# Batch norm with ReLU on one core: two-image tiles with 4 KB rows, or four tiles with 32 KB runs per partition

## The chip, the cores and the metric

The kernel runs on one core of one Trainium2 chip. The metric is the device time of one launch in microseconds (us), as the median over several runs. Beside that stands one profiled execution, whose span, from its first to its last instruction, is a little shorter than its device time.

## The reference

The input `x` has 32 images of 128 channels, each a plane of 32 by 32 float32 values (4 KB). Every channel has four parameters. In short:

```python
normalized = (x - running_mean[None, :, None, None]) / np.sqrt(running_var[None, :, None, None] + eps)
scaled = normalized * gamma[None, :, None, None] + beta[None, :, None, None]
return np.maximum(scaled, 0).astype(np.float32)
```

So each plane is multiplied by one number of its channel, another number of its channel is added, and negative values become zero. The input is 16.78 MB and the output is as large.

## The kernel before, in words

The 128 channels lie on the 128 partitions of the on-chip memory. A tile holds two images (1 MB, 8 KB per partition), and there are 16 tiles, all with a buffer of their own (`BUFS = 16`), so no load waits for a buffer. In DRAM one image is a block of 512 KB in which channel follows channel, so that a transfer of a tile moves 256 rows of 4 KB: two per partition, 512 KB apart, and neighbouring partitions are 4 KB apart.

Three queues issue transfers. GpSimd's (lines 63 to 66) brings the four parameter vectors, each as one row on one partition. The sync queue, SP, brings tile 0, in two halves, and then the tiles that ScalarE (ACT) does not bring: 2, 4, 6 and 8 to 15 (`emit_input`, line 58). ACT's own queue brings tiles 1, 3, 5 and 7 before ACT has anything to compute, and takes all the stores (lines 118 and 145). On a queue, transfers are issued in the order of the program; the Tile framework puts the waits on semaphores in, and hands the DMA semaphores out in turn, so that a transfer may also wait until an earlier one with the same semaphore has landed.

The parameter rows become columns through four small matmuls against a one (line 79). ACT takes the square root (line 89), and VectorE (DVE) makes from that the scale and the bias of each channel, as columns of 128 numbers (lines 97 to 103). Then the tiles go through ACT one by one: `relu(scale * x + bias)` in place, one instruction over both images of a tile (line 138), and its store behind it (line 145). Only tile 0 is done in three pieces (256 columns, 768 columns, then the second image; lines 109 and 118).

Of the kernel before, what the change touches and what calls it, by code (L numbers as in the profile page):

```python
# [1 line left out]

# [4 lines left out]


@with_exitstack
def kernel(  # L10
    ctx: ExitStack,
    tc: tile.TileContext,
    x: bass.AP,
    gamma: bass.AP,
    beta: bass.AP,
    running_mean: bass.AP,
    running_var: bass.AP,
    eps: bass.AP,
    out: bass.AP,
):  # L20
    nc = tc.nc

    B, C, H, W = x.shape
    HW = H * W
    assert C == nc.NUM_PARTITIONS, f"expected {nc.NUM_PARTITIONS} channels, got {C}"

    x3 = x.rearrange("b c h w -> b c (h w)")
    out3 = out.rearrange("b c h w -> b c (h w)")

    f32 = mybir.dt.float32  # L30

    NBMAX = 2
    n_tiles = B // NBMAX
    sizes = [NBMAX] * n_tiles
    scalar_tiles = (1, 3, 5, 7)
    splits = {0: 2, 1: 2}
    BUFS = 16
    SEPARATE_PSUM = True
    FIRST_PIECES = (256, HW - 256)

    params = ctx.enter_context(tc.tile_pool(name="params", bufs=1))
    eps_t = params.tile([C, 1], f32)
    nc.vector.memset(eps_t, float(eps))  # L43
    prow = params.tile([1, 4 * C], f32)
    one_t = params.tile([1, 1], f32)
    nc.vector.memset(one_t, 1.0)  # L46

    data = ctx.enter_context(tc.tile_pool(name="data", bufs=BUFS))
    tiles = {}
    for i in (0,) + scalar_tiles:  # L50
        tiles[i] = data.tile([C, NBMAX, HW], f32, name="t")

    def emit_input(i, t, engine):
        nsp = splits.get(i, 1)
        step = NBMAX // nsp
        b0 = i * NBMAX
        for j in range(nsp):
            engine.dma_start(  # L58
                out=t[:, j * step : (j + 1) * step],
                in_=x3[b0 + j * step : b0 + (j + 1) * step].transpose([1, 0, 2]),  # L60
            )

    nc.gpsimd.dma_start(out=prow[0:1, 3 * C : 4 * C], in_=running_var[None, :])  # L63
    nc.gpsimd.dma_start(out=prow[0:1, 0 * C : 1 * C], in_=gamma[None, :])  # L64
    nc.gpsimd.dma_start(out=prow[0:1, 2 * C : 3 * C], in_=running_mean[None, :])  # L65
    nc.gpsimd.dma_start(out=prow[0:1, 1 * C : 2 * C], in_=beta[None, :])  # L66

    emit_input(0, tiles[0], nc.sync)
    for i in scalar_tiles:
        emit_input(i, tiles[i], nc.scalar)  # L70

    pp = ctx.enter_context(tc.tile_pool(name="pp", bufs=1, space=bass.MemoryType.PSUM))
    if SEPARATE_PSUM:
        pcols = [pp.tile([C, 1], f32, name=f"p{k}") for k in range(4)]
    else:
        pc = pp.tile([C, 4], f32)
        pcols = [pc[:, k : k + 1] for k in range(4)]
    for k in (3, 0, 2, 1):
        nc.tensor.matmul(  # L79
            pcols[k],  # L80
            prow[0:1, k * C : (k + 1) * C],
            one_t[0:1, 0:1],
            start=True,
            stop=True,
        )
    g_col, b_col, mu_col, var_col = pcols

    std_t = params.tile([C, 1], f32)
    nc.scalar.activation(  # L89
        out=std_t,  # L90
        in_=var_col,
        func=mybir.ActivationFunctionType.Sqrt,
        bias=eps_t[:, 0:1],
        scale=1.0,
    )
    rstd_t = params.tile([C, 1], f32)
    nc.vector.reciprocal(out=rstd_t, in_=std_t)  # L97
    scale_t = params.tile([C, 1], f32)
    nc.vector.tensor_mul(out=scale_t, in0=g_col, in1=rstd_t)  # L99
    ms_t = params.tile([C, 1], f32)  # L100
    nc.vector.tensor_mul(out=ms_t, in0=mu_col, in1=scale_t)  # L101
    bias_t = params.tile([C, 1], f32)
    nc.vector.tensor_sub(out=bias_t, in0=b_col, in1=ms_t)  # L103

    out_ring = {}
    n_out = [0]

    def relu_store(t, b, img, c0, c1):
        nc.scalar.activation(  # L109
            out=t[:, img : img + 1, c0:c1],  # L110
            in_=t[:, img : img + 1, c0:c1],
            func=mybir.ActivationFunctionType.Relu,
            bias=bias_t[:, 0:1],
            scale=scale_t[:, 0:1],
        )
        eng = out_ring.get(n_out[0], nc.scalar)
        n_out[0] += 1
        eng.dma_start(
            out=out3[b : b + 1, :, c0:c1].transpose([1, 0, 2]),
            in_=t[:, img : img + 1, c0:c1],  # L120
        )

    for i, nb in enumerate(sizes):
        b0 = i * NBMAX
        if i in tiles:
            t = tiles.pop(i)
        else:
            t = data.tile([C, NBMAX, HW], f32, name="t")
            emit_input(i, t, nc.sync)
        if i == 0:  # L130
            c0 = 0
            for w in FIRST_PIECES:
                relu_store(t, b0, 0, c0, c0 + w)
                c0 += w
            for img in range(1, nb):
                relu_store(t, b0 + img, img, 0, HW)
        else:
            nc.scalar.activation(  # L138
                out=t[:, :nb],
                in_=t[:, :nb],  # L140
                func=mybir.ActivationFunctionType.Relu,
                bias=bias_t[:, 0:1],
                scale=scale_t[:, 0:1],
            )
            nc.scalar.dma_start(out=out3[b0 : b0 + nb].transpose([1, 0, 2]), in_=t[:, :nb])  # L145


# [1 line left out]
_INS = ['x', 'gamma', 'beta', 'running_mean', 'running_var', 'eps']  # L149
_OUTS = [((32, 128, 32, 32), 'float32')]  # L150
#: Inputs that are plain numbers.
_NUMBERS = {'eps': 1e-05}


# [26 lines left out]
```

## Time and profile before

| | |
|---|---|
| median of 16 runs | 86.61 us (86.34 to 87.12) |
| the profiled execution: device time | 86.48 us |
| the profiled execution: span | 84.7 us |
| read from DRAM, written to it | 16.78 MB, 16.78 MB |
| mean rate of the DMA engines over the span | 396 GB/s |
| ACT busy | 34.8 us (41%) |
| PE, DVE, POOL busy | 2.3, 0.7, 2.2 us |

The profile names engines: PE is TensorE, DVE is VectorE, ACT is ScalarE, POOL is GpSimd, SP is SyncE; a q behind a name means the sequencer of that engine, which issues transfers and handles waits. A core has 16 DMA engines. "DMA share" is the time that packets took in a stretch, divided by the stretch and by 16; it may exceed 1 where records of packets overlap. q1 is SP's queue, q10 that of ACT, q0 that of GpSimd, q14 brings instructions. "L138" is line 138 of the kernel.

### The profile page before, as it was taken

The numbers are of one execution on the slowest core, as the hardware profiler recorded it, in microseconds if no ns is written. First come the engines' busy times: TensorE is split into PE (matmuls) and PEld (weight loads), VectorE is DVE, ScalarE is ACT, GpSimd is POOL, SyncE is SP. The second block draws the span as 40 slices with busy tenths as digits, with TensorE's granted clock in tenths as the row PEclk, the third lists the DMA queues.
The fourth block names the chain that finished last, engine by engine and source line by source line (L and its number), as shares of the span: only waits on it lengthen the run. The fifth ranks groups of instructions, "written<-read, shape, count | busy, mean of one in ns | idle before, by whom it ended". The sixth has DMA issues, their size and how long they took to land.

```text
span 84.7 us, 153 instructions
## 1 busy us (share of the span) xinstructions
PE 2.3 (3%) x8; PEld 2.0 (2%) x8; DVE 0.7 (1%) x6; ACT 34.8 (41%) x20; POOL 2.2 (3%) x8
## 2 busy tenths in 40 slices
PE   0006400000000000000000000000000000000000
PEld 0005300000000000000000000000000000000000
DVE  0001100000000000000000000000000000000000
ACT  0321479006920890000039598693987920000000
POOL 5500000000000000000000000000000000000000
DMA  1999999999999999999999999999999999999991
GB/s 25 321 389 417 410 426 404 412 418 408 403 392 418 422 418 428 418 420 422 418 429 416 422 420 418 429 416 420 424 416 429 416 422 420 416 429 418 420 422 64
DMA packets 9025, 33.57 MB, mean 396 GB/s; under 512 B 704, under 2 KB 832, under 8 KB 9024
## 3 DMA queue, kind: packets, MB, share of 16 engines
q10 hardware_dynamic: 5616, 20.97, 60.9%
q1 hardware_dynamic: 3280, 12.58, 36.9%
q0 software_dynamic: 128, 0.00, 0.1%
q14 instruction: 1, 0.01, 0.0%
HBM read 16.78 MB, written 16.78 MB: 396 GB/s over the span
## 4 chain that ended last, share of the span: by engine, by line
DMA 65%; ACT 7%; ACTq 4%; issue 3%
DMA t<-in_x_dram 65%; ACT t L138 7%; ACTq L58 2%; ACTq L145 2%
## 5 line engine op out<-in xcount | busy, mean ns | idle before, releaser
L138 ACT ACTIVATE t<-t,bias_t,scale_t 128x2048 f32<-128x2048 f32 x15 | 30.6, 2085 | 24.8 <-DMA t<-in_x_dram 22.4
L109 ACT ACTIVATE t<-t,bias_t,scale_t 128x256 f32<-128x256 f32 (+2 forms) x3 | 2.8, 950 | 2.2 <-DVE bias_t L103 1.7
L89 ACT ACT_TABLE_LOAD x1 | 1.3, 1283 | 3.5 <-issue 3.5
L79 PE MATMUL p<-one_t,prow 1*128 1x1 f32 x8 | 2.3, 354 | 7.2 <-DMA prow<-in_running_var_dram 7.1
L79 PEld LDWEIGHTS p<-one_t,prow 1*128 1x128 f32 x8 | 2.0, 306 | 7.4 <-issue 7.1
L89 ACT ACTIVATE std_t<-p,eps_t 128x1 f32<-128x1 f32 x1 | 0.3, 262 | 2.9 <-PE p L79 2.9
L63 POOL DMA_DIRECT2D prow<-in_running_var_dram x1 | 0.6, 617 | 0.8 <-POOLq L162 0.8
L64 POOL DMA_DIRECT2D prow<-in_gamma_dram x1 | 0.5, 484 | 0.0
L65 POOL DMA_DIRECT2D prow<-in_running_mean_dram x1 | 0.5, 484 | 0.0
L66 POOL DMA_DIRECT2D prow<-in_beta_dram x1 | 0.5, 484 | 0.0
L97 DVE RECIPROCAL rstd_t<-std_t 128x1 f32<-128x1 f32 x1 | 0.2, 165 | 7.1 <-ACT std_t L89 7.1
L103 DVE TENSOR_TENSOR bias_t<-p,ms_t 128x1 f32<-128x1 f32 x1 | 0.2, 159 | 0.4 <-PE p L79 0.4
L101 DVE TENSOR_TENSOR ms_t<-p,scale_t 128x1 f32<-128x1 f32 x1 | 0.2, 157 | 0.5 <-PE p L79 0.5
L99 DVE TENSOR_TENSOR scale_t<-p,rstd_t 128x1 f32<-128x1 f32 x1 | 0.2, 159 | 0.1
L162 POOL MEMSET const-float32-0.0<- 128x1 f32 x1 | 0.1, 98 | 0.2 <-issue 0.2
L162 POOL MEMSET const-bfloat16-1.0<- 128x1 bf16 x1 | 0.1, 101 | 0.0
L162 POOL MEMSET const-float32-1.0<- 128x1 f32 x1 | 0.1, 98 | 0.0
L162 POOL MEMSET const-uint8-127<- 128x1 uint8 x1 | 0.1, 98 | 0.0
L43 DVE MEMSET eps_t<- 128x1 f32 x1 | 0.1, 59 | 0.8 <-PEq L162 0.8
L46 DVE MEMSET one_t<- 1x1 f32 x1 | 0.1, 59 | 0.0
## 6 DMA issues: line engine op xcount, KB each, us to landing
out_dram<-t ACTq DMA_DIRECT2D x15, 1024.0 KB, 15.0
t<-in_x_dram SPq DMA_DIRECT2D x11, 1024.0 KB, 17.5
t<-in_x_dram ACTq DMA_DIRECT2D x3, 1024.0 KB, 16.7
t<-in_x_dram SPq DMA_DIRECT2D x2, 512.0 KB, 6.1
t<-in_x_dram ACTq DMA_DIRECT2D x2, 512.0 KB, 6.4
out_dram<-t ACTq DMA_DIRECT2D x1, 512.0 KB, 10.8
out_dram<-t ACTq DMA_DIRECT2D x1, 384.0 KB, 16.4
out_dram<-t ACTq DMA_DIRECT2D x1, 128.0 KB, 15.4
```

The lines of the kernel that those rows point to most:

```text
L58: engine.dma_start(out=t[:, j * step : (j + 1) * step], in_=x3[b0 + j * step : b0 + (j + 1) * step].transpose([1, 0, 2]),)
L63: nc.gpsimd.dma_start(out=prow[0:1, 3 * C : 4 * C], in_=running_var[None, :])
L64: nc.gpsimd.dma_start(out=prow[0:1, 0 * C : 1 * C], in_=gamma[None, :])
L65: nc.gpsimd.dma_start(out=prow[0:1, 2 * C : 3 * C], in_=running_mean[None, :])
L66: nc.gpsimd.dma_start(out=prow[0:1, 1 * C : 2 * C], in_=beta[None, :])
L79: nc.tensor.matmul(pcols[k], prow[0:1, k * C : (k + 1) * C], one_t[0:1, 0:1], start=True, stop=True,)
L89: nc.scalar.activation(out=std_t, in_=var_col, func=mybir.ActivationFunctionType.Sqrt, bias=eps_t[:, 0:1], scale=1.0,)
L97: nc.vector.reciprocal(out=rstd_t, in_=std_t)
L109: nc.scalar.activation(out=t[:, img : img + 1, c0:c1], in_=t[:, img : img + 1, c0:c1], func=mybir.ActivationFunctionType.Relu, bias=bias_t ...
L138: nc.scalar.activation(out=t[:, :nb], in_=t[:, :nb], func=mybir.ActivationFunctionType.Relu, bias=bias_t[:, 0:1], scale=scale_t[:, 0:1],)
L145: nc.scalar.dma_start(out=out3[b0 : b0 + nb].transpose([1, 0, 2]), in_=t[:, :nb])
L162: nc = _bacc.Bacc("TRN2", target_bir_lowering=False, num_devices=1)
```

## The change

The tensor is seen as 4096 rows of 4 KB (image by image, channel by channel). A block of 2048 rows is dealt out so that each partition holds 16 neighbouring rows: partition p of block t holds rows 2048t + 16p to 2048t + 16p + 15, which are 64 KB in one piece of DRAM. There are two blocks, and each is handled in two pieces of 8 rows per partition. That makes four tiles of 4 MB, with one run of 32 KB per partition each; neighbouring partitions are 64 KB apart in DRAM. All four loads are issued first, all on SP's queue; the four stores are issued on SP's queue too, each behind the computation of its tile.

A partition now holds 16 different channels (8 of them in each tile), the same 16 for every eighth partition. So the scale and the bias are tables of 128 by 16. The four parameter vectors are loaded as 8 rows of 16 numbers on ACT's queue, one matmul against an 8 by 128 matrix of zeros and ones (built by GpSimd, lines 67 and 68) spreads them over the 128 partitions, and square root, reciprocal, multiplications and subtraction work on 16 columns. ACT then does one instruction per row index, 8 per tile and 32 in all, with a column of the tables each.

Beside that, there is a transfer on ACT's queue near the start, which writes zeros to the first 512 bytes of each of the 32 images of the output (`fill`). The stores write over them later.

The core of the diff; the lines taken out are the body of the function shown above:

```diff
+J = 16
+PIECES = ((0, 8), (8, 16))
...
+    xr = x.rearrange("b c h w -> (b c) (h w)").rearrange("(t p j) w -> t p j w", p=P, j=J)
+    outr = out.rearrange("b c h w -> (b c) (h w)").rearrange("(t p j) w -> t p j w", p=P, j=J)
...
+    tiles = []
+    for t in range(T):
+        for a, b in PIECES:
+            xt = data.tile([P, b - a, HW], F32, name=f"x{t}_{a}")
+            nc.sync.dma_start(out=xt, in_=xr[t, :, a:b, :])
+            tiles.append((t, a, b, xt))
+    fill = params.tile([B, 128], F32, name="fill")
+    nc.vector.memset(fill, 0.0)
+    nc.scalar.dma_start(out=out.rearrange("b c h w -> b (c h w)")[:, 0:128], in_=fill)
+    raw = params.tile([Q, 4, J], F32, name="raw")
+    for k, src in enumerate((running_var, gamma, running_mean, beta)):
+        nc.scalar.dma_start(out=raw[:, k, :], in_=src.rearrange("(q j) -> q j", j=J))
+    eps_t = params.tile([P, 1], F32, name="eps_t")
     nc.vector.memset(eps_t, float(eps))
+    rep = params.tile([Q, P // Q, Q], F32, name="rep")
+    nc.gpsimd.memset(rep, 1.0)
+    nc.gpsimd.affine_select(
...
+    cols = psum.tile([P, 4, J], F32, name="cols")
+    nc.tensor.matmul(
+        cols.rearrange("p k j -> p (k j)"),
+        rep.rearrange("q r s -> q (r s)"),
+        raw.rearrange("q k j -> q (k j)"),
...
+    nc.scalar.activation(out=std_t, in_=cols[:, 0, :], func=ACTF.Sqrt, bias=eps_t[:, 0:1], scale=1.0)
...
+    for t, a, b, xt in tiles:
+        for j in range(a, b):
+            nc.scalar.activation(
+                out=xt[:, j - a, :],
+                in_=xt[:, j - a, :],
+                func=ACTF.Relu,
+                bias=bias_t[:, j : j + 1],
+                scale=scale_t[:, j : j + 1],
             )
...
+        nc.sync.dma_start(out=outr[t, :, a:b, :], in_=xt)
```

On SP's queue the whole program is shown here as a difference, the lines before with a minus and those after with a plus (the number behind a tile's name tells its buffer; "x11" is eleven alike in a row; the branches are the program's ends):

```order
-L58 DMA t<-in_x_dram 128x1024 x2
-L58 DMA t<-in_x_dram 128x2x1024 x11
-L176 UNCONDITIONAL_BRANCH
+L136 UNCONDITIONAL_BRANCH
+L50 DMA x_0_64<-in_x_dram 128x8192
+L50 DMA x_8_66<-in_x_dram 128x8192
+L50 DMA x_0_68<-in_x_dram 128x8192
+L50 DMA x_8_70<-in_x_dram 128x8192
+L105 DMA out_dram<-x_0_64 128x8192
+L105 DMA out_dram<-x_8_66 128x8192
+L105 DMA out_dram<-x_0_68 128x8192
+L105 DMA out_dram<-x_8_70 128x8192
```

Thirteen loads of up to 1 MB have become four of 4 MB, and the stores, which ACT issued, now stand behind the loads on this queue.

On ACT, at the start of the program before, with the semaphores that each instruction waits for in brackets (DMAHW0 to 7 count landings of transfers, the others count instructions of an engine):

```order
1 L58 DMA t<-in_x_dram 128x1024 x2
2 L58 DMA t<-in_x_dram 128x2x1024 x3
3 L89 ACT_TABLE_LOAD
4 L89 ACTIVATE std_t<-p_88,eps_t 128x1 [waits PE_49]
5 L109 ACTIVATE t<-t,bias_t,scale_t 128x256 [waits DMAHW0_49,DVE_49]
6 L109 ACTIVATE t<-t,bias_t,scale_t 128x768
7 L118 DMA out_dram<-t 128x256 [waits DMAHW2_49,Activation_49]
8 L118 DMA out_dram<-t 128x768 [waits DMAHW3_49,Activation_49]
9 L109 ACTIVATE t<-t,bias_t,scale_t 128x1024
10 L138 ACTIVATE t<-t,bias_t,scale_t 128x2048 [waits DMAHW1_49]
```

And on ACT now, from its first transfer to the second tile:

```order
1 L63 DMA raw<-in_running_var_dram 8x16
2 L57 DMA out_dram<-fill 32x128 [waits DVE_49]
3 L63 DMA raw<-in_gamma_dram 8x16
4 L63 DMA raw<-in_running_mean_dram 8x16
5 L63 DMA raw<-in_beta_dram 8x16
6 L86 ACT_TABLE_LOAD [waits DVE_49]
7 L86 ACTIVATE std_t<-cols,eps_t 128x16 [waits PE_49]
8 L98 ACTIVATE x_0_64<-x_0_64,bias_t,scale_t 128x1024 [waits DMAHW1_49,DVE_49]
9 L98 ACTIVATE x_0_64<-x_0_64,bias_t,scale_t 128x1024 x7
10 L98 ACTIVATE x_8_66<-x_8_66,bias_t,scale_t 128x1024 [waits DMAHW6_49]
```

ACT's large loads are gone, five small transfers stand in their place, and between the activations there is no store any more.

On SP after the change the waits of the last load and of the stores are these (the order of SP with its semaphores, rows 3 to 8):

```order
3 L50 DMA x_0_68<-in_x_dram 128x8192
4 L50 DMA x_8_70<-in_x_dram 128x8192 [waits DMAHW0_49]
5 L105 DMA out_dram<-x_0_64 128x8192 [waits DMAHW2_49,DMAHW1_49,Activation_49]
6 L105 DMA out_dram<-x_8_66 128x8192 [waits DMAHW6_49,Activation_49]
7 L105 DMA out_dram<-x_0_68 128x8192 [waits DMAHW7_49,DMAHW3_49,Activation_49]
8 L105 DMA out_dram<-x_8_70 128x8192 [waits DMAHW4_49,DMAHW0_49,Activation_49]
```

The fourth load waits for one small transfer whose semaphore it takes over, and the first store waits for the fill, for the first load and for ACT.

More of the change, by code (lines that the diff above doesn't have):

```diff
@@ L6 @@
 from concourse._compat import with_exitstack
+F32 = mybir.dt.float32
+ACTF = mybir.ActivationFunctionType
+J = 16
+PIECES = ((0, 8), (8, 16))
 @with_exitstack
@@ L24 @@
     HW = H * W
[L25 to L39, printed above, removed]
-    params = ctx.enter_context(tc.tile_pool(name="params", bufs=1))
@@ L42 @@
-    eps_t = params.tile([C, 1], f32)
-    nc.vector.memset(eps_t, float(eps))
[L44 to L60, printed above, removed]
-            )
@@ L63 @@
[L63 to L145, printed above, removed]
+    P = nc.NUM_PARTITIONS
@@ new lines @@
+    assert C % J == 0 and P % (C // J) == 0 and (B * C) % (P * J) == 0
+    Q = C // J
+    T = B * C // (P * J)
+    xr = x.rearrange("b c h w -> (b c) (h w)").rearrange("(t p j) w -> t p j w", p=P, j=J)
+    outr = out.rearrange("b c h w -> (b c) (h w)").rearrange("(t p j) w -> t p j w", p=P, j=J)
+    data = ctx.enter_context(tc.tile_pool(name="data", bufs=1))
+    params = ctx.enter_context(tc.tile_pool(name="params", bufs=1))
+    psum = ctx.enter_context(tc.tile_pool(name="psum", bufs=1, space=bass.MemoryType.PSUM))
@@ new lines @@
+    eps_t = params.tile([P, 1], F32, name="eps_t")
+    nc.vector.memset(eps_t, float(eps))
+    rep = params.tile([Q, P // Q, Q], F32, name="rep")
+    nc.gpsimd.memset(rep, 1.0)
+    nc.gpsimd.affine_select(
+        out=rep,
+        in_=rep,
+        compare_op=mybir.AluOpType.is_equal,
+        fill=0.0,
+        base=0,
+        pattern=[[0, P // Q], [-1, Q]],
+        channel_multiplier=1,
+    )
+    cols = psum.tile([P, 4, J], F32, name="cols")
[3 more added lines that the diff above has]
+        raw.rearrange("q k j -> q (k j)"),
+        start=True,
+        stop=True,
+    )
@@ new lines @@
+    std_t = params.tile([P, J], F32, name="std_t")
+    nc.scalar.activation(out=std_t, in_=cols[:, 0, :], func=ACTF.Sqrt, bias=eps_t[:, 0:1], scale=1.0)
+    rstd_t = params.tile([P, J], F32, name="rstd_t")
+    nc.vector.reciprocal(out=rstd_t, in_=std_t)
+    scale_t = params.tile([P, J], F32, name="scale_t")
+    nc.vector.tensor_mul(out=scale_t, in0=cols[:, 1, :], in1=rstd_t)
+    ms_t = params.tile([P, J], F32, name="ms_t")
+    nc.vector.tensor_mul(out=ms_t, in0=cols[:, 2, :], in1=scale_t)
@@ L149 @@
+    bias_t = params.tile([P, J], F32, name="bias_t")
+    nc.vector.tensor_sub(out=bias_t, in0=cols[:, 3, :], in1=ms_t)
+    for t, a, b, xt in tiles:
[6 more added lines that the diff above has]
+                scale=scale_t[:, j : j + 1],
+            )
+        nc.sync.dma_start(out=outr[t, :, a:b, :], in_=xt)
 _INS = ['x', 'gamma', 'beta', 'running_mean', 'running_var', 'eps']
```

## The prediction

> **What bounds the kernel now.** I read the page first: its busy shares, its 40 slices and its queues.
>
> ```profile
> PE 2.3 (3%) x8; PEld 2.0 (2%) x8; DVE 0.7 (1%) x6; ACT 34.8 (41%) x20; POOL 2.2 (3%) x8
> DMA  1999999999999999999999999999999999999991
> GB/s 25 321 389 417 410 426 404 412 418 408 403 392 418 422 418 428 418 420 422 418 429 416 422 420 418 429 416 420 424 416 429 416 422 420 416 429 418 420 422 64
> q10 hardware_dynamic: 5616, 20.97, 60.9%
> q1 hardware_dynamic: 3280, 12.58, 36.9%
> ```
>
> No compute engine is busy for half of the span. The DMA engines are full in every slice but the first and the last: the kernel is a stream of 33.55 MB through 16 engines. A wait of ACT or SP matters only if it leaves the engines without work, and none does. So the next question is where the stream starts and ends, and how fast it is in between. This view cuts the span into stretches; the last two columns are the DMA share and GB/s.
>
> ```profile
> 0.00:1.85 1.85, 0.00 (x0) 0.00 (x0) 0.08 (x2) 0.00 (x0) 0.81 (x6) 1.00 0.00 0
> 1.85:5.00 3.15, 0.00 (x0) 0.00 (x0) 0.00 (x0) 1.28 (x1) 1.43 (x4) 1.00 0.94 321
> 5.00:23.00 18.00, 2.27 (x8) 1.98 (x8) 0.64 (x4) 8.18 (x7) 0.00 (x0) 1.00 1.03 411
> 23.00:27.00 4.00, 0.00 (x0) 0.00 (x0) 0.00 (x0) 0.90 (x1) 0.00 (x0) 1.00 1.04 406
> 27.00:60.00 33.00, 0.00 (x0) 0.00 (x0) 0.00 (x0) 17.18 (x9) 0.00 (x0) 1.00 1.02 421
> 60.00:83.20 23.20, 0.00 (x0) 0.00 (x0) 0.00 (x0) 7.28 (x4) 0.00 (x0) 1.00 1.01 415
> 83.20:84.70 1.50, 0.00 (x0) 0.00 (x0) 0.00 (x0) 0.00 (x0) 0.00 (x0) 1.00 0.00 0
> ```
>
> Nothing moves for 1.85 us, then the stream lasts 81.35 us, then 1.50 us pass until the program ends. Taking 421 GB/s as the full rate, the stream loses 3.15 x 100/421 = 0.75 us while it gets going, 22 us x 11/421 = 0.57 us between 5 and 27 us (about 410), and 23.2 x 6/421 = 0.33 us at the end, where the engines run out one after another. The remaining 79.7 us are 33.55 MB at 421.
>
> **What sets 421 GB/s.** Short windows in which a queue moves packets of one size give the price of a packet. Here are, with packets, MB and share of 16 engines, ACT's queue from 23.5 to 24.6 us (its packets under 2 KB are the 1 KB pieces of tile 0's first store, and one of 4 bytes), the same queue from 69.1 to 69.6 us (4 KB packets alone), and the instruction queue from 70.2 to 70.3 us, which moves one packet of 8 KB:
>
> ```profile
> DMA packets 173, 0.44 MB, mean 400 GB/s; under 512 B 1, under 2 KB 87, under 8 KB 173
> q10 hardware_dynamic: 87, 0.09, 22.6%
> q10 hardware_dynamic: 49, 0.20, 97.4%
> q14 instruction: 1, 0.01, 19.3%
> ```
>
> 1 KB: 0.226 x 16 x 1100 ns / 86 = 46.2 ns. 4 KB: 0.974 x 16 x 500 / 49 = 159.0 ns. 8 KB: 0.193 x 16 x 100 = 309 ns. The first two give 37.6 ns per KB and 8.6 ns per packet whatever its size; 8 KB by that would be 309.4 ns, and is 309. So a packet has a fixed part, and up to 8 KB it doesn't come back with size. In wall time it is smaller, because records overlap:
>
> ```profile
> DMA packets 3274, 12.62 MB, mean 421 GB/s; under 512 B 192, under 2 KB 192, under 8 KB 3274
> q10 hardware_dynamic: 1638, 6.32, 51.3%
> q1 hardware_dynamic: 1636, 6.31, 51.2%
> ```
>
> From 30 to 60 us, 3082 packets of 4 KB and 192 tiny ones use 16 x 30 us: 155.7 ns per 4 KB packet with its part of the tiny ones, about 155.3 without. The fixed part in wall time is thus 155.3 - 4 x 37.6 = 4.9 ns, 3% of the time.
>
> **The change part by part.** *32 KB runs.* If a run travels as one packet, it costs 8 x 150.4 + 4.9 = 1208 ns, or 1212 with the whole 8.6. Each engine then moves 64 runs in place of 512 rows: 64 x 1209 = 77.4 us (77.3 to 77.6) in place of 79.7. No packet above 8 KB is in this trace, so this reaches four times further than the rows; the bound on the other side is the packet price of today, 79.7 us, below as a rival.
>
> *Start and end.* SP issues its first load where it did, so 1.85 us stay, and 1.50 us at the end, where no line changes. Getting going: from 0 (long runs flow at once) to 0.75 us as now; I take 0.7, as today's row is the nearest. The end: engines run out within part of a run, 0 to 1.2 us; I take today's 0.3.
>
> *Loads first, then stores.* Until 23 us the kernel before only loads, at 411 GB/s, and from then on stores are mixed in, and it soon does 421. Now loads run alone for half the stream. If the slower loads are a matter of bytes, 36.7 us of stream lose 36.7 x 11/421 = 1.0 us; if of packets, an eighth, 0.1. I take 0.45.
>
> *Small transfers.* The fill is 32 pieces of 512 B, two per engine at 8.6 + 18.8 = 27 ns; the parameters are 32 pieces of 64 B at some 11 ns on some engines. With the packets that close a transfer I take 0.15 us (0.05 to 0.25).
>
> *The tables, hidden.* The small transfers share the engines with 32 KB runs. From 5.3 to 8.3 us three queues were active:
>
> ```profile
> q1 hardware_dynamic: 173, 0.63, 52.5%
> q10 hardware_dynamic: 163, 0.59, 48.8%
> q0 software_dynamic: 128, 0.00, 2.4%
> ```
>
> They take turns packet by packet, whatever the size (above, 86 packets of 4 KB beside 87 of mostly 1 KB say the same). q0's 128 packets for four transfers on 16 engines are two per transfer and engine, one with data, one that closes it. So ACT's five small transfers queue at most 11 packets on an engine (four of 2, and the fill with 3), each letting one run of 1.21 us pass: the last parameter lands at about 1.85 + 13.3 + 1 = 16 us (1 for the landing itself, since the 1.50 us at the program's end hold a landing and the shutdown). From the first matmul to the bias took 2.5 us:
>
> ```profile
> 7.11 2.33 PE L79 MATMUL p<-one_t,prow 1*128 1x1 f32 x8 [7.11 <-DMA prow<-in_running_var_dram]
> 9.48 0.16 DVE L103 TENSOR_TENSOR bias_t<-p,ms_t 128x1 f32<-128x1 f32 x1 [0.40 <-PE p L79]
> L109 ACT ACTIVATE t<-t,bias_t,scale_t 128x1024 f32<-128x1024 f32 x1 | 1.2, 1239 | 0.4 <-ACT t L109 0.4
> 0.74 13.39 SPq L58 DMA_DIRECT2D t<-in_x_dram  x6
> ```
>
> With one matmul in place of four and 16 columns in place of one I keep 2.5: tables at 19 us. A tile is 8 activations, at most 8 x 1.24 = 9.9 us: the tiles are ready at 29, 39, 49 and 59 us. The loads end at 1.85 + 0.7 + 0.45 + 38.7 = 41.7 us. A transfer issued to idle engines starts 1.1 us later (0.74 to 1.85), so store 0 is needed by 40.6, then one every 9.7 us: 50, 60, 69. The cover is 11 us at every store. GpSimd's two instructions for the matrix have until 16 us, when the last parameter lands, and work beside that. The fourth load waits on SP for running_var's landing, at about 5 us, with the stores queued behind it; three loads, 29 us of work, cover that. The first store waits for the fill, long landed.
>
> *Sum.* Stream: 77.4 + 0.7 + 0.45 + 0.15 + 0.3 = 79.0 us. Span: 1.85 + 79.0 + 1.50 = 82.35. The device time of the profiled execution is 86.48 - 84.7 = 1.78 us above its span, which gives 84.1 us against 86.48; the median is 0.13 above that execution, which I leave in the rounding.
>
> **The rivals.** *The runs are cut up, or long packets gain nothing* (the change doesn't do what it says): 79.7 us of payload return, with 0.75, 0.57 and 0.33, and the time is 86.4, no change. For it: no run over 8 KB was seen. Against: the 8 KB packet lies on the line. The Trainium skill, page "DMA: Bandwidth & Descriptors", section "Specifications", puts line rate at 512 bytes and above, by which 4 KB rows have nothing to gain. The 46.2 and 159.0 ns rows contradict that: per byte the 1 KB packet is 16% dearer. The same page, "Why small descriptors are slow (HBM only)", names a fixed cost of about 3 cycles per packet, which has the form the rows show.
>
> *Streams that collide in DRAM* (slower). Before, a transfer covers one or two solid blocks of 512 KB; now the engines walk at a time through runs that start multiples of 64 KB apart, up to 8 MB. If such starts share parts of the memory, every packet stretches. Break-even is 33.55 MB in 81.35 - 0.7 - 0.3 - 0.15 = 80.2 us, 418 GB/s. The worst full slice behind the start, 389, gives 86.2 us of payload, 87.4 of stream and 92.5 us. For it: loads are already slower than the rest, 411. Against: from 27 to 60 us loads and stores walk blocks far apart in two tensors at once, and the rate is a flat 421, which the packet price explains alone. The Trainium skill, same page, section "Latency and other measured facts", speaks against the change here: copies whose partitions lie 4 MiB apart run at half rate (103 of 214 GB/s), those 512 KiB apart at 207. At 64 KB the page lists nothing; the halving would make an estimate of some 163 us, and no run here shows any.
>
> *Tables too late* (slower). If the small packets let more than one run pass per turn, store 0 misses its slot. At two runs the last parameter lands at 29.5, tile 0 is ready at 41.9, 1.3 us late, 85.4 us. At three it is 55.2, 14.6 us late, 98.7 us. It decides at just above two. For it: no row has a small packet beside long ones. Against: the turns above are one by one for 1 KB beside 4 KB and 32 bytes beside 4 KB.
>
> **How the numbers follow.** Forecast 0.76: 84.1 us, with own bounds, in the order of the sum, of 82.6 (77.3, 0, 0.1, 0.05, 0) to 85.9 (77.6, 0.75, 1.0, 0.25, 1.2). Cut or no gain 0.10: 86.4. Collisions 0.08: about 92.5. Late tables 0.04: 85 to 99. The rest, 0.02, I leave to what I don't see. The range is 82.6 to 86.4: the forecast and the case of no gain, about 0.82. A measurement of this kernel can tell about 0.2%, 0.17 us, from no change. Faster by more: the forecast and a third of the no-gain case, whose tiny packets also shrink in number, 0.79. Within: 0.07. Slower: 0.14, collisions, late tables and the rest.
>
> **What would show it.** Right: the queue table has some 1024 packets of 32 KB on SP's queue, priced near 1212 ns; the slices show about 433 GB/s in the store half and 422 to 433 in the load half; the first data packet is at 1.85 us and no slice between is empty; tables by 19 us; the first store issued near 29 us. Wrong: packets of 4 KB again, a rate of 421 or under, a hole near 42 us, or ACT still at work when its store's turn comes.

## The result, and the profile after

The change makes the kernel about 2% faster: 84.78 us (9 runs, 84.56 to 84.93) against 86.58 (48 runs), a ratio of 0.9785 with a 95% interval of 0.9769 to 0.9801. Forecast were 84.1 us in a range of 82.6 to 86.4. The profiled execution took 85.04 us with a span of 83.3.

From the page of the kernel after, the DMA row of the slices, its rate and the queues (packets, MB, share of 16 engines):

```profile
DMA  7789998998999799899879999999999999989970
GB/s 189 299 363 415 488 425 346 503 488 362 409 503 456 315 488 488 377 393 503 252 330 425 488 409 393 472 456 409 393 488 409 409 456 488 393 377 488 456 315 0
q1 hardware_dynamic: 1152, 33.55, 95.5%
q10 hardware_dynamic: 112, 0.02, 0.1%
```

The 8320 data packets of 4 KB and less have become 1024 of 32 KB with 128 small ones that close the eight transfers. A packet now lasts over half a slice and its bytes count where it starts, so the rate jumps between slices; only the dip in the two at 40 to 44 us (252, 330) is more than that. Longer stretches are steadier (last two columns: DMA share, GB/s):

```profile
0.00:1.80 1.80, 0.00 (x0) 0.00 (x0) 0.17 (x2) 0.00 (x0) 0.79 (x6) 1.00 0.00 0
1.80:5.00 3.20, 0.00 (x0) 0.00 (x0) 0.00 (x0) 1.28 (x1) 0.00 (x0) 1.00 1.10 389
5.00:38.00 33.00, 0.66 (x2) 0.50 (x2) 0.78 (x4) 20.50 (x19) 0.00 (x0) 1.00 1.01 437
38.00:44.00 6.00, 0.00 (x0) 0.00 (x0) 0.00 (x0) 6.00 (x7) 0.00 (x0) 1.00 0.95 322
44.00:80.00 36.00, 0.00 (x0) 0.00 (x0) 0.00 (x0) 10.07 (x9) 0.00 (x0) 1.00 1.00 432
82.00:83.30 1.30, 0.00 (x0) 0.00 (x0) 0.00 (x0) 0.00 (x0) 0.00 (x0) 1.00 0.00 0
```

The stream runs from 1.8 to 82.0 us, 80.2 us in place of 81.35. Loads, up to 38 us, and stores, behind 44, both move about 433 GB/s (437 and 432, with packets counted where they start); between them the rate falls to 322. The price of a packet there comes from SP's queue in three windows: 1.8 to 5 us, 38 to 44 and 44 to 80 (16 of the 75 packets and 48 of the 523 are the small ones, at 9 ns):

```profile
q1 hardware_dynamic: 38, 1.25, 109.9%
q1 hardware_dynamic: 75, 1.93, 94.8%
q1 hardware_dynamic: 523, 15.56, 100.1%
```

From 44 to 80 us, 475 long packets share 1.001 x 16 x 36 = 576.6 us: 1.213 us each. From 38 to 44 us, 59 long packets have 91.0 us where they should need 71.6: 19.3 us more, or 1.2 us on each of the 16 engines. I call this surplus over the regular price, per engine, the loss of a stretch. Followed packet by packet, it sits in the last two load runs of every engine (numbers 31 and 32 of 32), 1.2 to 2.2 us long and 1.8 in the mean; the first store run behind them has the regular price. At the start, 38 packets lose 0.64 us per engine in the same way.

The tables, from the timeline of after:

```profile
15.78 0.66 PE L78 MATMUL cols<-raw,rep 8*128 8x64 f32 x2 [15.78 <-DMA raw<-in_beta_dram]
17.77 36.30 ACT L98 ACTIVATE x<-x,bias_t,scale_t 128x1024 f32<-128x1024 f32 x32 [1.02 <-DVE bias_t L94]
26.95 27.48 SPq L105 DMA_DIRECT2D out_dram<-x  x4
```

The last parameter landed at 15.8 us and the tables were there at 17.8, late beside the 9.7 of before but without harm: the first store was issued at 26.95 us, and the engines began it at about 42.

### The profile page after: what moved, and what is told of

It is laid out like the page before. It is cut to its first block, busy times and chain, and to the rows that moved or that the text cites. A ratio compares the mean times of both kernels' runs of the same rounds, so it can differ in the third digit from the quotient of the medians.

```text
span 83.3 us, 117 instructions
## 1 busy us (share of the span) xinstructions
PE 0.7 (1%) x2; PEld 0.5 (1%) x2; DVE 1.0 (1%) x6; ACT 37.9 (45%) x34; POOL 0.8 (1%) x6
## 4 chain that ended last, share of the span: by engine, by line
ACT 43%; DMA 16%; ACTq 3%; DVE 1%; PE 1%; issue 1%; DVEq 0%
ACT x L98 42%; DMA raw<-in_beta_dram 16%; ACTq L63 2%; ACTq L136 1%; PE cols L78 1%; ACTq L57 0%; ACT std_t L86 0%; DVE rstd_t L88 0%; DVE ms_t L92 0%; DVE scale_t L90 0%; DVE bias_t L94 0%; DVEq L90 0%
## 5 line engine op out<-in xcount | busy, mean ns | idle before, releaser
L98 ACT ACTIVATE x<-x,bias_t,scale_t 128x1024 f32<-128x1024 f32 x32 | 36.3, 1226 | 1.0 <-DVE bias_t L94 1.0
L78 PE MATMUL cols<-raw,rep 8*128 8x64 f32 x2 | 0.7, 428 | 15.8 <-DMA raw<-in_beta_dram 15.8
L78 PEld LDWEIGHTS cols<-raw,rep 8*128 8x128 f32 x2 | 0.5, 308 | 15.7 <-issue 15.7
```

The source lines that it names most:

```text
L78: nc.tensor.matmul(cols.rearrange("p k j -> p (k j)"), rep.rearrange("q r s -> q (r s)"), raw.rearrange("q k j -> q (k j)"), start=True, s ...
L98: nc.scalar.activation(out=xt[:, j - a, :], in_=xt[:, j - a, :], func=ACTF.Relu, bias=bias_t[:, j : j + 1], scale=scale_t[:, j : j + 1],)
```

## The experiments

Each kernel is the one after the change with one edit. Its time is a median, its ratio is to the kernel before on the same chip.

**e1: without the early zeros.** Is the loss near 40 us the price of touching the output first, which the zeros might lower?

```diff
-    nc.scalar.dma_start(out=out.rearrange("b c h w -> b (c h w)")[:, 0:128], in_=fill)
```

> The early transfer of zeros is left out, nothing else. After the change each DMA engine's first two store packets take 1.8 us instead of 1.21, about 1.2 us in all, near 39 us. Theory 'first touch' (the first writes to the output are slow whoever makes them, and the zeros take part of that cost early): without the zeros the first store packets get dearer by some 0.5 us or more, and the time goes from 84.8 to 85.3 or more. Theory 'turn' (an engine that goes from loads to stores with nothing else to do pays for the change of direction): the zeros do nothing for it, the first two packets stay at 1.8 us and the time at 84.6 to 84.8. Both expect the tables some 3.6 us earlier (three packets fewer on ACT's queue ahead of beta, each behind a run of 1.21 us), at no gain in time.

84.75 us, ratio 0.9767 (0.9730 to 0.9803): nothing lost, nothing gained, where "first touch" expected 85.3 or more. (The expectation takes the slow runs for stores; they are the last loads, as said above.) From 38 to 44 us its SP queue shows:

```profile
q1 hardware_dynamic: 78, 2.03, 100.2%
```

62 long packets have 96.2 us against 75.2: 1.3 us per engine, as with the zeros. The zeros are dead weight.

**e2: 4 KB packets, all else kept.** A gap of 16 bytes behind each row in the tile cuts the runs.

```diff
-            xt = data.tile([P, b - a, HW], F32, name=f"x{t}_{a}")
+            xt = data.tile([P, b - a, HW + 4], F32, name=f"x{t}_{a}")[:, :, 0:HW]
```

> Each 4 KB row gets 16 bytes of padding in the on-chip tile, so that a partition's 32 KB are moved as 8 packets of 4 KB; addresses in DRAM, transfers, queues and tables stay. Theory 'packet price' (the prediction's: 4.9 ns of wall time per packet): 512 packets per engine in place of 64 cost 448 x 4.9 ns = 2.2 us more, so 87.0 us, slower than the kernel before, and the store half runs at 421 GB/s. Rival (the gain comes from the single queue, the pattern of 64 KB in DRAM or the order, not from run length): 84.8 us again. Both expect the table to be ready earlier, as the small packets pass 4 KB packets.

86.46 us, ratio 0.9962 (0.9939 to 0.9985). On the same chip e1 took 84.75 us, so run length is worth 1.7 us. Everything else together (single queue, order, tables) is worth the rest, 0.3 us by this ratio (0.1 to 0.5). Packets and rates of e2 from 10 to 38, 38 to 44 and 44 to 80 us, each as a total and as SP's queue:

```profile
DMA packets 2859, 11.51 MB, mean 411 GB/s; under 512 B 48, under 2 KB 48, under 8 KB 2859
q1 hardware_dynamic: 2859, 11.51, 102.5%
q1 hardware_dynamic: 622, 2.48, 102.6%
DMA packets 3753, 15.18 MB, mean 422 GB/s; under 512 B 48, under 2 KB 48, under 8 KB 3753
```

Stores do 422, the packet price, as forecast. Loads do 411: 2811 packets of 4 KB have 459.2 us against 446.9 at 159 ns, a loss of 0.75 us spread over the load half. But the 1.2 us before the first store are missing (0.1 between 38 and 44). So the sum is 84.78 + 2.2 + 0.75 - 1.1 = 86.6, near the 86.46 measured; my 87.0 had counted on the loss staying.

**e3: more changes between loads and stores.** The fourth load goes behind the first store.

```diff
         nc.sync.dma_start(out=outr[t, :, a:b, :], in_=xt)
+        if n == 0:
+            lt, la, lb, lx = tiles[3]
+            nc.sync.dma_start(out=lx, in_=xr[lt, :, la:lb, :])
```

> The fourth load is issued behind the first store: three loads, store, load, three stores, all on SP's queue. That makes three changes of direction in place of one. Theory 'turn': two changes from loads to stores at 1.2 us each and one back, of 0 to 0.7 us: time 86.0 to 86.7, with slow packets near 31 us, near 41 us and near 51 us. Theory 'first touch': only the first store pays, now near 31 us, and the time stays at 84.8.

85.01 us, ratio 0.9793 (0.9755 to 0.9831), 0.2 us above "first touch" and 1 below "turn". SP's queue from 28 to 34 us, the first change, and from 48 to 54, the last one:

```profile
q1 hardware_dynamic: 78, 2.03, 97.7%
q1 hardware_dynamic: 96, 2.62, 101.7%
```

The first change loses 1.15 us per engine (62 long packets), the last one 0.03 (80). "Turn" falls: the price is paid once, wherever the first store comes. "First touch" had that right, but e1 speaks against it, the slow packets are loads, and e8 below will speak against it too.

**e4: stores on ACT's queue.** Engines then take turns between a load run and a store run.

```diff
-        nc.sync.dma_start(out=outr[t, :, a:b, :], in_=xt)
+        nc.scalar.dma_start(out=outr[t, :, a:b, :], in_=xt)
```

> The stores go to ACT's queue, loads stay on SP's. From about 28 us on an engine then takes turns between a load run and a store run, as the kernel before did with its 4 KB rows. Theory 'turn': a store's slow start lies beside load packets of the other queue, the 1.2 us are hidden at least by half, time 83.6 to 84.2. Theory 'first touch': the first store packets hold the engine just as long, time 84.7 to 84.9. ACT has its four store issues of some 0.4 us more to do, which is covered.

85.34 us, ratio 0.9826 (0.9785 to 0.9867), slower than either theory gave. The loss is not hidden behind the other queue's packets (27 to 32 us; q1 loads, q10 the first stores):

```profile
q1 hardware_dynamic: 36, 1.18, 75.7%
q10 hardware_dynamic: 13, 0.43, 19.7%
```

49 long packets have 76.3 us against 59.4, 1.05 per engine. It is unevenly spread here: three engines have a single load run of 2.8 to 3.2 us. Followed to the end, the same three finish last, at 81.7, 82.1 and 82.3 us, and the other 13 by 81.25; in the kernel after the last one ends at 82.0. So these three make the stream 0.4 us longer, of the 0.6 by which the profiled execution is above that of the kernel after (85.64 against 85.04); the rest stays open.

**e6: short packets in the first store.** Tile 0 is stored as eight transfers of 4 KB rows.

```diff
+        if t == 0 and a == 0:
+            for r in range(a, b):
+                nc.sync.dma_start(out=outr[t, :, r, :], in_=xt[:, r - a, :])
+        else:
+            nc.sync.dma_start(out=outr[t, :, a:b, :], in_=xt)
```

> The store of the first tile goes out as eight transfers of one 4 KB row per partition; everything else keeps its 32 KB runs. So far: on every engine the last two load runs ahead of the first store take 1.8 us in place of 1.21 (about 1.2 us in all); the first store itself runs at full price; a later change from loads to stores costs nothing; 4 KB packets show no such stretch. Theory 'read ahead by packets' (an engine starts to read the next two packets while the last loads still arrive, and what it reads early is two whole runs): with 4 KB packets behind the loads the stretch shrinks to 0.3 us or less, at 0.3 us more for the packet price of 64 short packets: 83.9 to 84.2 us. Theory 'once' (the first store of the program costs 1.2 us whatever its packets are): 85.0 to 85.1 us, and the last two load runs are as slow as before.

85.10 us, ratio 0.9824 (0.9808 to 0.9839): "once". From 38 to 42.3 us SP's queue of e6 has

```profile
q1 hardware_dynamic: 32, 1.05, 82.6%
```

32 load runs at 0.826 x 16 x 4.3 / 32 = 1.78 us in the mean, exactly two per engine. The size of the store's packets doesn't matter.

**e8: a full-size store early.** One run of 32 KB of zeros per engine replaces the short rows.

```diff
-    fill = params.tile([B, 128], F32, name="fill")
+    fill = params.tile([16, 8192], F32, name="fill")
...
+    nc.scalar.dma_start(out=outr[0, 0:16, 0:8, :].rearrange("p j w -> p (j w)"), in_=fill)
```

> In place of the 32 short rows the early transfer writes one run of 32 KB of zeros per engine (16 partitions), behind the parameters on ACT's queue, so a full-size store passes each engine before 16 us. It moves 0.52 MB more, 1.21 us per engine. Theory 'once' (each engine pays 1.2 us the first time that a long store stands behind loads, and never again): slow load runs before 16 us, none near 39 us, time 84.8 + 1.2 = 86.0 us. Theory 'turn' (an engine that has been loading alone pays at the turn): the stretch near 39 us stays at 1.1 to 1.3 us, and the early one may come on top: 86.0 to 87.2 us. The place of the slow packets tells them apart more than the time.

86.46 us, ratio 0.9997 (0.9981 to 1.0013). Its queues from 11 to 17 us (q10 is the zeros), and SP's from 38 to 44:

```profile
q1 hardware_dynamic: 59, 1.41, 57.2%
q10 hardware_dynamic: 28, 0.52, 44.6%
q1 hardware_dynamic: 84, 2.62, 101.1%
```

The loss has moved: 59 long packets (28 are small) lose 1.6 us per engine at 11 to 17 us, and between 38 and 44 us 80 runs lose nothing. Most of it falls on the run of zeros itself, 0.446 x 96 / 16 = 2.7 us each, and less on the loads. The place is what "once" expected, the time 0.4 us above. The zeros lie on 16 partitions alone, and whether that adds to their 2.7 us wasn't tested; that the loss near 40 us is gone doesn't depend on it.

**e12: an early store of 4 KB per engine.**

```diff
-    fill = params.tile([B, 128], F32, name="fill")
+    fill = params.tile([16, 1024], F32, name="fill")
...
+    nc.scalar.dma_start(out=outr[0, 0:16, 0, :], in_=fill)
```

> The early transfer writes one row of 4 KB of zeros per engine (16 partitions), against one run of 32 KB in the run with the big early store, where the stretch moved to 13 us and was gone at 39, and against two pieces of 512 bytes, with which it stays at 39. Theory 'any real store' (one packet of a store opens the way, whatever its size): the stretch moves ahead of 16 us and is gone at 39 us, same sum, 84.8 to 85.1 us. Theory 'amount' (as many bytes have to be read for stores as the stretch is worth, some 32 KB per engine): about an eighth of it moves, the rest stays near 39 us, 84.8 to 85.0 us. The place tells them apart, not the time.

84.85 us, ratio 0.9794 (0.9768 to 0.9820). SP's queue from 38 to 44 us:

```profile
q1 hardware_dynamic: 74, 1.90, 96.3%
```

1.37 us per engine (58 long packets): 4 KB per engine buy nothing off, so it isn't the first store packet as such. (The eight packets of zeros near 6 us and the eight near 11 have the regular 159 ns.)

**e10: short packets just ahead of the first store.** The last row of the last load is a transfer of its own.

```diff
+                nc.sync.dma_start(out=xt[:, 0:7, :], in_=xr[t, :, a : b - 1, :])
+                nc.sync.dma_start(out=xt[:, 7, :], in_=xr[t, :, b - 1, :])
```

> The last load is cut in two: rows 8 to 14 of a partition (28 KB runs), then row 15 alone as a transfer of its own (4 KB, 8 packets per engine, the last ones before the first store). Known so far: the 1.2 us before the first store are paid once, by the last two load runs on each engine, and do not depend on the size of the store's packets; with 4 KB and 8 KB runs everywhere nothing of the kind is seen. Theory 'load runs' (what is stretched is the last two load packets, in proportion to their size): with 4 KB packets there, the stretch falls to 0.2 us or less, at 8 x 4.9 ns for the packets: 83.6 to 83.9 us. Theory 'amount' (the first store costs a fixed 1.2 us behind long runs, wherever it falls): the 8 short packets or the runs ahead of them are stretched by as much in all, 84.7 to 84.9 us.

85.12 us, ratio 0.9812 (0.9784 to 0.9840). SP's queue from 39 to 44 us moves 17 packets of 32 KB, 16 of 28, 128 of 4 and 32 small ones, 58.2 us at regular prices:

```profile
q1 hardware_dynamic: 193, 1.54, 101.5%
```

They have 81.2 us: 1.4 per engine. Now a 28 KB run and, on average, three packets of 4 KB per engine are stretched, the latter from 0.16 to some 0.5 us. The loss is an amount, not a share of the packet, and the time is 0.2 us above what "amount" gave.

**e9 and e11: 8 KB and 16 KB packets throughout**, by the gap of e2 behind every two or four rows.

```diff
-            xt = data.tile([P, b - a, HW], F32, name=f"x{t}_{a}")
+            xp = data.tile([P, (b - a) // 2, 2 * HW + 4], F32, name=f"x{t}_{a}")
+            xt = xp[:, :, 0 : 2 * HW]
```

> 16 bytes of padding behind every two rows: packets of 8 KB, 256 per engine. With 4 KB packets (e2) loads alone ran at 411 GB/s and stores at 422; with 32 KB both run at 433. By the packet price alone (4.9 ns each): 256 x 305.7 = 78.3 us of payload in place of 77.4, and both halves at 428. Theory 'the slower loads are a matter of packets': the loads reach 425 to 428 too, and if the stretch before the first store grows with the packet (a quarter of 1.2 us, or none as with 4 KB), the time is 84.8 + 0.9 - 0.9 to 84.8 + 0.9 - 1.2 = 84.5 to 84.8 us. Rival (loads lose 2.5% per byte below some larger size, and the stretch stays): 86.0 to 86.7 us.

> 16 bytes of padding behind every four rows: packets of 16 KB, 128 per engine; 128 x 606.5 = 77.6 us of payload against 77.4. With 8 KB runs loads ran at 422, stores at 428, with no stretch before the first store. If the load rate follows the packet size (about 428 alone, stores 431) and the stretch is absent: 84.8 + 0.2 + 0.5 - 1.2 = 84.3 us. If the stretch is there at half its size (0.6 us): 84.9 us. If it is there in full: 85.3 to 85.5 us.

84.82 us (0.9794, 0.9778 to 0.9810) and 84.80 us (0.9790, 0.9762 to 0.9818): the same as 32 KB. That is the upper edge of what "a matter of packets" gave for e9, and near the case of half a stretch for e11. e9 from 14 to 38 us and from 44 to 80:

```profile
DMA packets 1271, 10.15 MB, mean 423 GB/s; under 512 B 32, under 2 KB 32, under 8 KB 32
q1 hardware_dynamic: 1271, 10.15, 101.2%
DMA packets 1930, 15.42 MB, mean 428 GB/s; under 512 B 48, under 2 KB 48, under 8 KB 48
```

and e11 from 14 to 38 us and from 38 to 44:

```profile
DMA packets 659, 10.27 MB, mean 428 GB/s; under 512 B 32, under 2 KB 32, under 8 KB 32
q1 hardware_dynamic: 157, 2.31, 102.4%
```

Put side by side, loss per engine in the load half and around the first store: 4 KB 0.75 and 0.1 us, 8 KB 0.35 and 0.1, 16 KB 0.1 and 0.75, 32 KB 0.0 and 1.2. Short load packets pay on the way, long ones pay at the first store, and the longer packet's lower price is eaten up by that.

The loss on the way doesn't begin with the loads. SP's queue early in the load half, in e2 from 5 to 8 us, e9 from 6 to 13.5 and e11 from 6 to 24, and then late in it, e11 from 28 to 38:

```profile
q1 hardware_dynamic: 302, 1.24, 100.0%
q1 hardware_dynamic: 407, 3.20, 100.8%
q1 hardware_dynamic: 501, 7.68, 99.6%
q1 hardware_dynamic: 275, 4.24, 99.8%
```

Without the small ones (0, 16, 32 and 16) these are 159.0, 309.0, 611.0 and 616 ns per packet: regular at first, then 5 ns dearer. In all three sizes the price is regular up to about the 38th packet of each engine and higher from about the 40th on, which is at 9, 14.5 and 26 us, and it stays some 2 to 6 ns higher (averaged over 64 packets) until the first store. So with packets of one size this part goes by their number, not by bytes or time; with 32 KB an engine has 32 loads in all and never gets there. The number alone isn't the whole rule: in e13 below, where 32 packets of 8 KB follow 24 of 32 KB, the price is still regular at the 49th.

**e13 and e14: 8 KB for loads, 32 KB for stores.** The gap is only in the loads' destination; the activations write each row to its place without gaps. e14 does it for all loads, e13 for the last one.

```diff
+            nc.sync.dma_start(
+                out=xt.rearrange("p (g w) -> p g w", g=4)[:, :, 0 : 2 * HW],
+                in_=xr[t, :, a:b, :].rearrange("p (g r) w -> p g (r w)", r=2),
+            )
...
+            src0 = (j - a) * HW + 4 * ((j - a) // 2)
...
+                out=xt[:, (j - a) * HW : (j - a + 1) * HW],
+                in_=xt[:, src0 : src0 + HW],
```

> The first three loads keep 32 KB runs, the last one is cut into packets of 8 KB (a gap of 16 bytes behind every two rows on the chip, closed by the activations, so that all stores keep 32 KB runs). Time lost to stretched packets per engine so far, between 5 and 38 us and around the first store: 0.75 and 0.12 us with 4 KB runs, 0.35 and 0.08 with 8 KB, 0.08 and 0.75 with 16 KB, 0.01 and 1.20 with 32 KB. Theory 'what stands before the store' (the stretch depends on the size of the loads that are under way when the first store comes): with 8 KB packets there it falls to about 0.1 to 0.2 us, 83.8 to 84.0 us. Theory 'debt' (long loads leave something to be made up that the first store calls in, whatever the last packets are): the stretch stays above 0.8 us, spread over several 8 KB packets, 84.6 to 84.9 us.

> All loads in 8 KB packets, all stores in 32 KB runs, by the same gap that the activations close. Expected from the runs so far: loads at 422 GB/s with 0.35 us lost on the way, the first store nearly free (0.1 us), stores at 433. Against the change as it is: 128 x (4 x 305.7 - 1208)/4 ns, 0.4 us dearer for loads, and 0.43 us lost in place of 1.21: 84.4 us. This may be the fastest form of the kernel. If the stretch comes from long stores after all, 1.2 us stay: 85.5 us.

e13: 84.61 us, ratio 0.9775 (0.9756 to 0.9794). Its SP queue from 38 to 44 us:

```profile
q1 hardware_dynamic: 223, 2.43, 108.5%
```

These are 177 packets of 8 KB, 30 of 32 KB and 16 small ones, which lose 0.8 us per engine. That is at the edge of what "debt" expected and far from 0.1 to 0.2: the packets under way are not alone in setting it. e14: 84.42 us (84.34 to 84.48), ratio 0.9756 (0.9737 to 0.9775), as its sum had it. From 14 to 38 us and from 44 to 80:

```profile
DMA packets 1269, 10.13 MB, mean 422 GB/s; under 512 B 32, under 2 KB 32, under 8 KB 32
DMA packets 526, 15.66 MB, mean 435 GB/s; under 512 B 48, under 2 KB 48, under 8 KB 48
```

This is the fastest form found, 0.4 us below the kernel after the change, though the two intervals of the ratio still touch (0.9769 and 0.9775).

## Why the prediction was right

The range alone was no hard test, since it reached up to no change; 0.7 us of the 2.5 that were forecast as a gain didn't come. What carries the prediction is the price of a packet.

- **The bound and the packet price** held. 32 KB runs travel as one packet each, at 1.213 us, where 1.212 was worked out from packets of 1, 4 and 8 KB; e2 shows that the gain is theirs.
- **Start and end** held in part: 1.8 us before the stream; 0.64 us lost in getting going, for 0.7; behind the stream 1.3 us, for 1.5. What is left of the stream, 0.8 us (80.2 less 77.4, 0.64, 1.2 and 0.15), I put on the engines running out at the end, for 0.3, inside the bounds of 0 to 1.2; they end between 81.1 and 82.0 us, which shows 0.55 us of it on average.
- **Loads first, then stores** is the step that failed. It put 0.45 us on slower loads, 0.1 to 1.0. At 32 KB the loads lose nothing on the way, close to the 0.1 of its case "of packets". But 1.2 us that it had no term for are paid at once before the first store, just beyond the bound. That loads were at 411 GB/s until 23 us in the kernel before, and at 421 behind it, beside stores, is the loss of 4 KB loads on the way, as in e2 (411, then 422). This term and the end make up the stream's 1.16 us over the forecast; the shorter end and the gap between span and device time (1.7 us) give 0.2 back. That explains 85.04 us, the profiled execution; the median is 0.26 below it.
- **The tables** were hidden as worked out: beta at 15.8 us for 16, tables at 17.8 for 19. One run let past per small packet holds, but that the sum came out so near is partly luck: of the 11 packets two left before the stream began (1.75 us), one fell beside the small packet that closes the first load (12.3 us), and the first of the others had to let three runs pass (6.1 us); the other seven are 1.2 us apart. The first store came at 27 us for 29, as the tables were 1.2 us earlier and an activation behind another takes 36.30/32 = 1.13 us, not 1.24.
- **The rivals**: runs were not cut; streams 64 KB apart don't collide (433 GB/s in both halves). By the Trainium skill, page "DMA: Bandwidth & Descriptors", section "Specifications", 4 KB rows would have been at line rate already; e2 against the kernel after, 86.46 and 84.78 us, decides against that. Late tables didn't happen; in e1, with three small packets fewer ahead of beta, ACT began on the first tile at 15.2 us in place of 17.8 (2.6 us earlier, for 3.6 expected), and the kernel took as long.

**What stays open** is what the engines do in those 1.2 us. The runs show that the loss falls once, on the load packets ahead of the first sizable store (in e8 on that store too), that 32 KB of stores per engine settle it and 4 KB don't, and that it is 0.1 us where all loads are of 4 or 8 KB, which lose time on the way instead. That the one loss is paid in place of the other is only argued: the two don't add up to the same (0.85, 0.45, 0.85 and 1.2 us), and in e13 the loads lose nothing on the way and 0.8 us are left at the store. That reads for the first stores begin while loads are still under way would fit the stretched loads, but not the count of some forty packets; no run shows it.

## What to carry to other kernels

Where all DMA engines are busy, divide a window's share by its packets: a fixed part per packet is then visible, and the run length in both memories is the lever (here 3% at 4 KB). Sum loads and stores apart, and expect the first large store behind a stretch of loads to cost about a microsecond once, where the loads are in runs of 16 or 32 KB; 8 KB loads with 32 KB stores gave up least. A preparatory transfer such as the zeros here should be taken out once to see what it does: here it did nothing for the time.

## What the runs showed of the hardware that wasn't expected

Loads alone run slower per packet than stores (411 against 422 GB/s at 4 KB, 423 against 428 at 8 KB, no difference at 32 KB), or than loads once stores have begun (421 at 4 KB in the kernel before). This begins at about the 40th packet of an engine in each of three sizes, and adds some 2 to 6 ns per packet. The first large store stretches the packets around it by 0.75 us per engine at 16 KB and by 1.05 to 1.6 us at 32 KB, and a later change from loads to stores doesn't (0.03 us in e3).
